# A transformer layer on one core: the second product's weight sums loaded into other buffers, the first pairs' vector work and the last row tiles put in another order

## The chip, the cores and the metric

The kernel runs on one core of a Trainium2 chip. A core has a matrix engine (TensorE, PE in the profile, with its weight loads as PEld), a vector engine (VectorE, DVE), an engine for activations and copies (ScalarE, ACT), a general engine (GpSimd, POOL) and a queue engine (SyncE, SP) that here only issues DMAs. Each engine carries out its own list of instructions strictly in the order in which they were put there; engines wait for each other on semaphores. The metric is the device time of one execution in microseconds.

## The reference

One encoder layer over 512 positions of width 1024, all in float32. A normed input goes through one large projection, a gMLP branch and a dilated attention branch, both merged through gates and an output projection, with a residual. Then comes the feed-forward part, which is where the change lies:

```python
n2 = rms_norm(h, norm_mlp_pre[l])
hid = jnp.square(jax.nn.relu(jnp.einsum('bsd,df->bsf', n2, w_up[l])))
mlp_out = jnp.einsum('bsf,fd->bsd', hid, w_down[l])
h = h + rms_norm(mlp_out, norm_mlp_post[l])
```

`w_up` is 1024 x 4096 and `w_down` is 4096 x 1024. The output is h, 512 x 1024.

## The kernel before, in words

**Float32 by three products.** The matrix engine works on a rounded float32 type. Each operand is split into a high part, a rounded copy made by ScalarE (line 79), and a low part, the difference, made by VectorE (line 80; both in `split_into`). A product of two split operands is three matmuls: high x high, high x low, low x high (`mm3`, `acc3`, and the loop in `product`). So each operand costs one ACT and one DVE pass before PE may use it.

**Seven products in place of eight.** Most of the work is done on 2 x 2 blocks by a seven-product scheme (Winograd's form): sums and differences of blocks are made on VectorE, seven block products run on PE, and results are combined ("joined") on VectorE out of the accumulators. PE saves an eighth of the work, VectorE gets more of it.

**The up projection** (lines 878 to 1006). The normed rows of row tile t are transposed and split by `turn(t)`; its last DVE instruction is returned, and the one of the last call is `turned`. Two pairs of 128-wide feature tiles are computed in the plain way (`up_half`, lines 850 and 922 to 926). The other pairs, i = 2 to 15, use seven products. The four block sums of the moving operand (lines 934 to 937) and their splits `nt[2]`, `nt[1]`, `nt[3]`, `nt[4]` (line 941) are made once; the low part of `nt[4]` is made by GpSimd, the others by VectorE. For each pair, `prep(i)` loads 1 MB of weights into a two-deep ring (`raw_up`, line 911), makes sums in the tile `s` (lines 948, 949, 954; one buffer) and splits `s12`, `ar`, `a12`, `s34`. Then the loop issues the products 6, (the previous pair's 4, in `tail`), 1, 5, 2, 7, 3. Product 7 needs `nt[3]`, product 4 needs `nt[4]`, product 2 needs `a12`, products 1 and 4 need `ar`. Accumulators are copied out or joined at lines 987 to 1005. The last join of the stage is the DVE instruction at line 1002 of the last pair's `tail`.

**The down projection** (from line 1009). The 32 hidden tiles are the contraction. Tiles 0 to 15 are done plainly, two at a time by `plain(f2, order)`: 1 MB of `w_down` into the ring `dnw` of two buffers (tag `raw`, the same ring as the up weights), two splits of it into the ring `hl` of five buffers, 48 matmuls. Tiles 16 to 31 form two chunks c for the seven-product scheme. Order in the code: `plain(0)`, `plain(1)`, `plain(2)`, `first_sums(0)`, `plain(3)`, `first_sums(1)`, `plain(4)`, then the products on chunks, `plain(5)` to `plain(7)`, more products. `first_sums(c)` loads two weight blocks of 1 MB each through the same ring (`block`, line 1052), writes their difference into `tsum[c]` by two DVE instructions (line 1083, in `two`), and makes two sums of hidden blocks (lines 1088 and 1090). `two` serves at lines 1109 and 1171 too, where `tsum[c]` gets further sums.

**The end** (lines 1161 to 1189). The last chunk's products finish row tiles 2 and 3 (accumulators Y) and 0 and 1 (X), 12 matmuls per row tile. For each, `finish` squares with a running sum on ACT (line 1158; the square itself is thrown away into the output tile `o`), multiplies by the gain on DVE (1159), forms the root on GpSimd (96), and writes `o` by two DVE instructions (1153) and two DMAs (1155). The pool of `o` has two buffers, so that the tiles of rows 0 and 1 take over those of rows 2 and 3. The pool `n2pool` has eight buffers of 4 KB per partition: the early moving operands, and behind them `gain`, `s2`, `v`, `t1` and `h2`.

**Who sets the order.** The program is written in one order, and a planner with its own cost estimates picks for each engine, among the instructions that it takes to be ready, the one that stands first in the program. `tc.issue_after(x)` forces instructions of the block that run on x's engine to stand behind x in that engine's list; it adds no wait between engines and does not touch DMAs that another engine issues. Buffers of a pool are handed to a new tile when the planner has seen the old one freed, and the first write then waits for the last reader.

Of the kernel before, what the change touches and what calls it, by code (L numbers as in the profile page):

```python
# [36 lines left out]
def block_kernel(ctx: ExitStack, tc: tile.TileContext, x, norm_mix_pre, w_in, b_gate, ln_v_gain, ln_v_bias,  # L37
# [40 lines left out]
    def split_into(hi, lo, src, sub=nc.vector):  # L78
        nc.scalar.activation(hi, src, AF.Copy)  # L79
        return sub.tensor_tensor(lo, src, hi.bitcast(F32), op=ALU.subtract)  # L80
# [775 lines left out]
    for t in range(4):  # L856
# [18 lines left out]
        r = rstd_of(ss, 1.0 / D)  # L875
        for hs in halves:
            nc.scalar.activation(xn[:, hs], h2[:, hs], AF.Copy, scale=r)
    stds = []
    for w in early:
        stds.append((psB.tile([P, S], F32, name="pu", tag="acc", bufs=4), *w))  # L880
        with tc.issue_after(final.ins):
            final = up_half(*stds[-1], 0)
        with tc.issue_after(final.ins):
            turned = turn(len(stds) + 1)
    wo.close()
    rst.close()
    mst.close()
# [45 lines left out]
    with tc.issue_after(turned.ins):  # L933
        nc.vector.tensor_tensor(fe[:, :, A], fe[:, :, A], fe[:, :, B], op=ALU.subtract)
        nc.vector.tensor_tensor(fe[:, :, B], fo[:, :, B], fe[:, :, B], op=ALU.subtract)
        nc.vector.scalar_tensor_tensor(fo[:, :, B], fe[:, :, A], -1.0, fo[:, :, B], op0=ALU.mult, op1=ALU.subtract)
        nc.vector.scalar_tensor_tensor(fo[:, :, A], fo[:, :, B], -1.0, fo[:, :, A], op0=ALU.mult, op1=ALU.subtract)
        nt = {}
        for nm, src in ((2, fo[:, :, B]), (1, fe[:, :, A]), (3, fe[:, :, B]), (4, fo[:, :, A])):
            nt[nm] = [n2_tile() if nm == 4 else tpool.tile([P, KH, 256], F32R, name="nt", tag="nt") for _ in range(2)]  # L940
            split_into(*nt[nm], src, nc.gpsimd if nm == 4 else nc.vector)
    hst.close()
    hidb = pool(back, "hidb", side="right")

    def prep(i):
        raw = raw_up(i).rearrange("p (j h) (r c) -> p j (h r) c", h=2, r=2)
        s = upool.tile([P, KH, 4, P], F32, name="s", bufs=1)
        nc.vector.tensor_tensor(s[:, :, 0:4:2], raw[:, :, 1:3], raw[:, :, 0:1].to_broadcast([P, KH, 2, P]), op=ALU.add)
        nc.vector.tensor_tensor(s[:, :, 3], s[:, :, 2], raw[:, :, 1], op=ALU.add)  # L949
        s12 = split_back(s[:, :, 2:4], [KH, 2, P])  # L950
        ar = split_back(raw[:, :, 1:3], [KH, 2, P])
        a12 = [upool.tile([P, KH, P], F32R, name="a12" + z) for z in "hl"]
        split_into(*a12, raw[:, :, 3])
        nc.vector.tensor_tensor(s[:, :, 1], s[:, :, 3], raw[:, :, 3], op=ALU.add)
        s34 = split_back(s[:, :, 0:2], [KH, 2, P])
        pick = lambda g, m: [z[:, :, m] for z in g]
        return {1: pick(ar, 0), 2: a12, 3: pick(s34, 1), 4: pick(ar, 1), 5: pick(s12, 0), 6: pick(s12, 1), 7: pick(s34, 0)}
# [16 lines left out]
    for i in range(NSTD, KF // 2):  # L974
# [1 line left out]
        if f % 8 == 0:  # L976
            hid.append((hida if f < 24 else hidb).tile([P, 8, S], F32, name="hid"))
        c2, c1 = hid_of(f), hid_of(f + 1)
        with nullcontext() if i > NSTD else tc.issue_after(turned.ins):
            w = prep(i)  # L980
        Y, Z, X = half_bank("acc"), half_bank("acc"), half_bank("tp")
        product(6, Y, w, True)
        if tail:
# [15 lines left out]

        def tail(w=w, Y=Y, p1=p1, c2=c2, f=f):  # L1000
            product(4, Y, w, False)
            nc.vector.scalar_tensor_tensor(c2[:, :256], Y, -1.0, p1, op0=ALU.mult, op1=ALU.subtract)
            both = hid[f // 8][:, f % 8:f % 8 + 2]
            nc.scalar.activation(both, both, AF.Relu)
            nc.scalar.activation(both, both, AF.Square)
    tail()
    up.close()

    dpool = pool(dn, "dpool", bufs=3)
# [69 lines left out]
    s2 = []  # L1079

    def two(out, x, y, op):
        for i in range(0, 4, 2):
            nc.vector.tensor_tensor(out[:, i:i + 2], x[:, i:i + 2], y[:, i:i + 2], op=op)

    def first_sums(c):
        b22, b12 = block(c, 1, 1), block(c, 0, 1)
        two(tsum[c], b22, b12, ALU.subtract)
        nc.vector.tensor_tensor(a21[c], a11[c], a21[c], op=ALU.subtract)
        s2.append(n2pool.tile([P, 4, 256], F32, name="s2", tag="n2"))
        nc.vector.tensor_tensor(s2[c], a22[c], a21[c], op=ALU.subtract)  # L1090

    first_sums(0)
    plain(3, order)
    first_sums(1)
    plain(4, y_first)
    keep = hida.tile([P, 8, S], F32, name="hid")
    p1, r22, r12, z0 = [keep[:, 2 * i:2 * i + 2] for i in range(4)]
# [71 lines left out]
    for c in range(2):  # L1169
        b21 = block(c, 1, 0)  # L1170
        two(tsum[c], b21, tsum[c], ALU.subtract)
        h4, w4 = h_split(a22[c]), w_split(tsum[c])
        h, w = h_split(a12[c]), w_split(b21)
        if c:
            break
        for i in range(2):
            piece(Y, h4, w4, i)
            piece(X, h, w, i)
    for ps, (hh, hl), ws, ts in ((Y, h4, w4, (2, 3)), (X, h, w, (0, 1))):
        for t in range(2):  # L1180
            for j in range(4):
                wh, wl = ws[j // 2]
                acc3(ps[t], (hh[:, j, tsl[t]], hl[:, j, tsl[t]]), (wh[:, j % 2], wl[:, j % 2]), False, j == 3)
            o = lpool.tile([P, D], F32, name="o")
            if ps is Y:
                nc.vector.tensor_tensor(p1[:, t], Y[t], p1[:, t], op=ALU.add)
                finish(2 + t, [p1[:, t], None], [p1[:, t], r22[:, t]], o, sums[2 + t])
# [45 lines left out]
```

## Time and profile before

| | us |
|---|---|
| three timed runs | 800.35, 801.00, 801.66 (median 801.0) |
| the profiled execution | 800.84 |
| its span, first to last instruction | 799.0 |
| PE busy | 782.7 (98%) |
| DVE busy | 590.9 (74%) |
| ACT busy | 441.9 (55%) |
| POOL busy | 60.4 (8%) |
| granted TensorE clock, mean | 0.995 |

Times in the views are microseconds from the start of the span. A row of the timeline gives start, duration, engine, line, operation, output<-inputs, shapes and how many instructions were merged; what stands in brackets is how long the engine was idle before and what ended that. A row of a DMA-issuing queue (SPq) gives the issue, not the transfer. Matmul rows overlap, since matmuls are pipelined: a 512-column matmul is listed with 0.39 us, and a new one starts every 0.23 us.

### The profile page before, as it was taken

The page shows a single profiled execution, that of the slowest core. Times are in us where ns is not written, and L with a number is a line of the kernel's source. Part 1 is how long each engine was busy: PE and PEld are TensorE (multiplying, and loading weights), DVE is VectorE, ACT ScalarE, POOL GpSimd, SP SyncE. Part 2 cuts the span into 40 slices and gives each one's busy share as a digit, 9 for nine tenths or more (in the row PEclk, how much of TensorE's full clock was granted, in tenths as well). Part 3 has the DMA queues.
Part 4 walks back from the last instruction along what each step waited for, and adds up shares of the span by engine and source line. Part 5 has one row for each costly group of instructions (what it writes and reads, how often), then busy time and mean ns, then how long its engine had stood idle before and what let it go on. Part 6 is the DMA issues. An engine that isn't in the chain of part 4 may idle for free.

```text
span 799.0 us, 12247 instructions
## 1 busy us (share of the span) xinstructions
PE 782.7 (98%) x4869; PEld 710.5 (89%) x4869; DVE 590.9 (74%) x956; ACT 441.9 (55%) x731; POOL 60.4 (8%) x86
## 2 busy tenths in 40 slices
PE   9999999999999999999999999999999999999994
PEld 6899999998988889999988899999999887888883
DVE  6784679978664878788656489988888546896686
ACT  6351467978686554455435457666667424543551
POOL 2300100010104400000001102000000000000001
PEclk9999999999999999999999999999999999999998
DMA  9633733352525433353356222433333354233302
GB/s 324 220 108 107 209 106 106 83 156 75 174 96 137 140 80 107 81 147 89 132 185 202 89 80 82 131 106 106 107 106 129 109 210 159 71 141 131 132 1 105
DMA packets 93706, 101.01 MB, mean 126 GB/s; under 512 B 2721, under 2 KB 74433, under 8 KB 93650
## 3 DMA queue, kind: packets, MB, share of 16 engines
q1 hardware_dynamic: 83312, 79.70, 32.0%
q0 software_dynamic: 10336, 20.54, 8.4%
q8 instruction: 38, 0.62, 0.3%
q14 instruction: 18, 0.15, 0.1%
q10 hardware_dynamic: 2, 0.00, 0.0%
HBM read 90.27 MB, written 9.96 MB: 125 GB/s over the span
## 4 chain that ended last, share of the span: by engine, by line
PE 88%; DVE 5%; DMA 3%; ACT 2%; issue 1%; POOL 0%; DVEq 0%; POOLq 0%; ACTq 0%
PE pacc L965 12%; PE pg L343 9%; PE pgacc L343 6%; PE pd L1032 5%; PE pd L1033 5%; PE pf L84 5%; PE pd L1034 5%; PE pf L85 5%; PE pf L86 5%; PE ptp L965 5%; PE pv L84 4%; PE pv L86 4%; PE pv L85 4%; PE pgS L343 3%; DMA dnw<-in_w_down_dram 2%; PE pd L86 2%
## 5 line engine op out<-in xcount | busy, mean ns | idle before, releaser
L1033 PE MATMUL pd<-hl,hhl 128*128 128x512 f32 x240 | 93.2, 389 | 0.0
L1034 PE MATMUL pd<-hl,hhl 128*128 128x512 f32 x240 | 91.3, 389 | 0.0
L1032 PE MATMUL pd<-hl,hhl 128*128 128x512 f32 x240 | 88.7, 390 | 1.6 <-ACT hl L79 1.6
L965 PE MATMUL pacc<-nt,hl 128*128 128x256 f32 x504 | 66.7, 279 | 1.4 <-DVE nt L80 1.4
L965 PEld LDWEIGHTS pacc<-nt,hl 128*128 128x128 f32 x504 | 62.2, 188 | 1.6 <-DVE nt L80 1.6
L1032 PEld LDWEIGHTS pd<-hl,hhl 128*128 128x128 f32 x240 | 45.0, 188 | 11.2 <-ACT hl L79 2.0
L1034 PEld LDWEIGHTS pd<-hl,hhl 128*128 128x128 f32 x240 | 45.1, 188 | 9.4
L1033 PEld LDWEIGHTS pd<-hl,hhl 128*128 128x128 f32 x240 | 45.1, 188 | 9.2
L79 ACT ACTIVATE hl<-dnw 128x1024 fp32r<-128x1024 f32 x28 | 29.3, 1054 | 41.0 <-PE pd L1034 17.1
L80 DVE TENSOR_TENSOR hl<-dnw,hl 128x1024 fp32r<-128x1024 f32 x28 | 33.9, 1222 | 16.0 <-ACT hl L79 16.0
L74 ACT ACTIVATE hi<-s 128x1024 fp32r<-128x1024 f32 x30 | 31.7, 1059 | 23.8 <-DVE s L330 10.4
L965 PE MATMUL pacc<-n,hl 128*128 128x256 f32 x336 | 44.7, 279 | 0.0
L84 PE MATMUL pf<-nh,hi 128*128 128x512 f32 x112 | 44.5, 397 | 0.0
L85 PE MATMUL pf<-nl,hi 128*128 128x512 f32 x112 | 43.9, 392 | 0.0
L86 PE MATMUL pf<-nh,lo 128*128 128x512 f32 x112 | 43.9, 392 | 0.0
L75 DVE TENSOR_TENSOR lo<-s,hi 128x1024 fp32r<-128x1024 f32 x30 | 36.6, 1223 | 9.7 <-ACT hi L74 9.6
L965 PEld LDWEIGHTS pacc<-n,hl 128*128 128x128 f32 x336 | 41.7, 188 | 0.1
L79 ACT ACTIVATE hl<-s 128x1024 fp32r<-128x1024 f32 x28 | 29.6, 1056 | 21.9 <-DVE s L949 15.6
L80 DVE TENSOR_TENSOR hl<-s,hl 128x1024 fp32r<-128x1024 f32 x28 | 34.2, 1221 | 6.2 <-ACT hl L79 6.2
L85 PE MATMUL pv<-lo,nh 128*128 128x512 f32 x96 | 38.2, 397 | 0.0
L86 PE MATMUL pv<-hi,nl 128*128 128x512 f32 x96 | 37.6, 396 | 0.0
L84 PE MATMUL pv<-hi,nh 128*128 128x512 f32 x96 | 37.4, 397 | 0.0
(387 smaller groups left out, 2221.2 us busy)
## 6 DMA issues: line engine op xcount, KB each, us to landing
dnw<-in_w_down_dram SPq DMA_DIRECT2D x18, 1024.0 KB, 4.8
upw<-in_w_up_dram SPq DMA_DIRECT2D x16, 1024.0 KB, 5.5
qkw<-in_w_in_dram SPq DMA_DIRECT2D x24, 512.0 KB, 5.2
gw<-in_w_in_dram SPq DMA_DIRECT2D x16, 512.0 KB, 5.3
slab<-in_w_in_dram SPq DMA_DIRECT2D x6, 1024.0 KB, 8.8
wow<-in_w_out_dram SPq DMA_DIRECT2D x4, 1024.0 KB, 4.9
w0raw<-in_w_in_dram SPq DMA_DIRECT2D x4, 512.0 KB, 6.4
v0d<-v POOLq DMA_DIRECT2D x4, 512.0 KB, 4.5
```

The costliest lines, as they stand in the source:

```text
L74: nc.scalar.activation(hi, raw, AF.Copy)
L75: (sub or nc.vector).tensor_tensor(lo, raw, hi.bitcast(F32), op=ALU.subtract)
L79: nc.scalar.activation(hi, src, AF.Copy)
L80: return sub.tensor_tensor(lo, src, hi.bitcast(F32), op=ALU.subtract)
L84: nc.tensor.matmul(ps, ah, bh, start=start, stop=False)
L85: nc.tensor.matmul(ps, ah, bl, start=False, stop=False)
L86: return nc.tensor.matmul(ps, al, bh, start=False, stop=stop)
L343: nc.tensor.matmul(ps, a[:, j], b[:, j], start=first and not (j or i), stop=(j == KH - 1 and i == 2), skip_group_check=True)
L965: nc.tensor.matmul(ps, a[:, j], b[:, j], start=first and not (j or m), stop=(j == KH - 1 and m == 2), skip_group_check=True)
L1032: nc.tensor.matmul(ps, ah, bh, start=start, stop=False, skip_group_check=True)
L1033: nc.tensor.matmul(ps, ah, bl, start=False, stop=False, skip_group_check=True)
L1034: return nc.tensor.matmul(ps, al, bh, start=False, stop=stop, skip_group_check=True)
```

## The change

Four edits, in the order of the program.

1. The start of the seven-product up projection. The first sum of the first such pair (line 948, i = 2) may stand on DVE as early as behind the first of the two late `turn` calls; the rest of its `prep` stays behind the second. All DVE work of pair 3's `prep` stands behind the low part of `nt[3]`. For pairs 3 and 4 the split of `ar` is written ahead of that of `s12`. The low part of `nt[4]` is made by VectorE.
2. `first_sums`: one weight block is loaded straight into `tsum[c]`, the other in two halves into two tiles of `n2pool`; neither passes through the `dnw` ring. All its DVE instructions are placed behind the last join of the up projection. The DMAs are issued by SP and are not placed by this.
3. `two` is one DVE instruction over 2048 columns per partition where there were two over 1024.
4. The end: the 12 matmuls of each row tile of the last chunk stand behind those of the row tile before (rows 2, 3, 0, 1), and the output tiles of rows 0 and 1 come from `n2pool`.

```diff
--- before.py
+++ after.py
@@ -875,13 +875,14 @@
         r = rstd_of(ss, 1.0 / D)
         for hs in halves:
             nc.scalar.activation(xn[:, hs], h2[:, hs], AF.Copy, scale=r)
-    stds = []
+    stds, turns = [], []
     for w in early:
         stds.append((psB.tile([P, S], F32, name="pu", tag="acc", bufs=4), *w))
         with tc.issue_after(final.ins):
             final = up_half(*stds[-1], 0)
         with tc.issue_after(final.ins):
-            turned = turn(len(stds) + 1)
+            turns.append(turn(len(stds) + 1))
+    turned = turns[-1]
     wo.close()
     rst.close()
     mst.close()
@@ -938,17 +939,25 @@
         nt = {}
         for nm, src in ((2, fo[:, :, B]), (1, fe[:, :, A]), (3, fe[:, :, B]), (4, fo[:, :, A])):
             nt[nm] = [n2_tile() if nm == 4 else tpool.tile([P, KH, 256], F32R, name="nt", tag="nt") for _ in range(2)]
-            split_into(*nt[nm], src, nc.gpsimd if nm == 4 else nc.vector)
+            low = split_into(*nt[nm], src)
+            if nm == 3:
+                low3 = low
     hst.close()
     hidb = pool(back, "hidb", side="right")
 
     def prep(i):
         raw = raw_up(i).rearrange("p (j h) (r c) -> p j (h r) c", h=2, r=2)
         s = upool.tile([P, KH, 4, P], F32, name="s", bufs=1)
-        nc.vector.tensor_tensor(s[:, :, 0:4:2], raw[:, :, 1:3], raw[:, :, 0:1].to_broadcast([P, KH, 2, P]), op=ALU.add)
+        with tc.issue_after((turns[0] if i == NSTD else low3).ins) if i < NSTD + 2 else nullcontext():
+            nc.vector.tensor_tensor(s[:, :, 0:4:2], raw[:, :, 1:3], raw[:, :, 0:1].to_broadcast([P, KH, 2, P]), op=ALU.add)
+        with tc.issue_after((turned if i == NSTD else low3).ins) if i < NSTD + 2 else nullcontext():
+            return prep_rest(raw, s, NSTD < i < NSTD + 3)
+
+    def prep_rest(raw, s, ar_first):
+        ar = split_back(raw[:, :, 1:3], [KH, 2, P]) if ar_first else None
         nc.vector.tensor_tensor(s[:, :, 3], s[:, :, 2], raw[:, :, 1], op=ALU.add)
         s12 = split_back(s[:, :, 2:4], [KH, 2, P])
-        ar = split_back(raw[:, :, 1:3], [KH, 2, P])
+        ar = ar or split_back(raw[:, :, 1:3], [KH, 2, P])
         a12 = [upool.tile([P, KH, P], F32R, name="a12" + z) for z in "hl"]
         split_into(*a12, raw[:, :, 3])
         nc.vector.tensor_tensor(s[:, :, 1], s[:, :, 3], raw[:, :, 3], op=ALU.add)
@@ -976,8 +985,7 @@
         if f % 8 == 0:
             hid.append((hida if f < 24 else hidb).tile([P, 8, S], F32, name="hid"))
         c2, c1 = hid_of(f), hid_of(f + 1)
-        with nullcontext() if i > NSTD else tc.issue_after(turned.ins):
-            w = prep(i)
+        w = prep(i)
         Y, Z, X = half_bank("acc"), half_bank("acc"), half_bank("tp")
         product(6, Y, w, True)
         if tail:
@@ -999,11 +1007,12 @@
 
         def tail(w=w, Y=Y, p1=p1, c2=c2, f=f):
             product(4, Y, w, False)
-            nc.vector.scalar_tensor_tensor(c2[:, :256], Y, -1.0, p1, op0=ALU.mult, op1=ALU.subtract)
+            joined = nc.vector.scalar_tensor_tensor(c2[:, :256], Y, -1.0, p1, op0=ALU.mult, op1=ALU.subtract)
             both = hid[f // 8][:, f % 8:f % 8 + 2]
             nc.scalar.activation(both, both, AF.Relu)
             nc.scalar.activation(both, both, AF.Square)
-    tail()
+            return joined
+    joined = tail()
     up.close()
 
     dpool = pool(dn, "dpool", bufs=3)
@@ -1079,19 +1088,23 @@
     s2 = []
 
     def two(out, x, y, op):
+        nc.vector.tensor_tensor(out, x, y, op=op)
+
+    def first_sums(c):
+        nc.sync.dma_start(tsum[c], w7[c, 0, :, :, halves[1]])
         for i in range(0, 4, 2):
-            nc.vector.tensor_tensor(out[:, i:i + 2], x[:, i:i + 2], y[:, i:i + 2], op=op)
-
-    def first_sums(c):
-        b22, b12 = block(c, 1, 1), block(c, 0, 1)
-        two(tsum[c], b22, b12, ALU.subtract)
+            b22 = n2pool.tile([P, 2, 512], F32, name="b22", tag="n2")
+            nc.sync.dma_start(b22, w7[c, 1, :, i:i + 2, halves[1]])
+            nc.vector.tensor_tensor(tsum[c][:, i:i + 2], b22, tsum[c][:, i:i + 2], op=ALU.subtract)
         nc.vector.tensor_tensor(a21[c], a11[c], a21[c], op=ALU.subtract)
         s2.append(n2pool.tile([P, 4, 256], F32, name="s2", tag="n2"))
         nc.vector.tensor_tensor(s2[c], a22[c], a21[c], op=ALU.subtract)
 
-    first_sums(0)
+    with tc.issue_after(joined.ins):
+        first_sums(0)
     plain(3, order)
-    first_sums(1)
+    with tc.issue_after(joined.ins):
+        first_sums(1)
     plain(4, y_first)
     keep = hida.tile([P, 8, S], F32, name="hid")
     p1, r22, r12, z0 = [keep[:, 2 * i:2 * i + 2] for i in range(4)]
@@ -1176,12 +1189,14 @@
         for i in range(2):
             piece(Y, h4, w4, i)
             piece(X, h, w, i)
+    final = None
     for ps, (hh, hl), ws, ts in ((Y, h4, w4, (2, 3)), (X, h, w, (0, 1))):
         for t in range(2):
-            for j in range(4):
-                wh, wl = ws[j // 2]
-                acc3(ps[t], (hh[:, j, tsl[t]], hl[:, j, tsl[t]]), (wh[:, j % 2], wl[:, j % 2]), False, j == 3)
-            o = lpool.tile([P, D], F32, name="o")
+            with tc.issue_after(final.ins) if final else nullcontext():
+                for j in range(4):
+                    wh, wl = ws[j // 2]
+                    final = acc3(ps[t], (hh[:, j, tsl[t]], hl[:, j, tsl[t]]), (wh[:, j % 2], wl[:, j % 2]), False, j == 3)
+            o = lpool.tile([P, D], F32, name="o") if ps is Y else n2pool.tile([P, D], F32, name="o2", tag="n2")
             if ps is Y:
                 nc.vector.tensor_tensor(p1[:, t], Y[t], p1[:, t], op=ALU.add)
                 finish(2 + t, [p1[:, t], None], [p1[:, t], r22[:, t]], o, sums[2 + t])
```

## The prediction

> **What bounds the kernel now.** I read first the page, then the list of what the matrix engine waited for, then the timeline around the few places that this list names. Page and list:
>
> ```profile
> span 799.0 us, 12247 instructions
> PE 782.7 (98%) x4869; PEld 710.5 (89%) x4869; DVE 590.9 (74%) x956; ACT 441.9 (55%) x731; POOL 60.4 (8%) x86
> ...
> PE pd L1032 <- ACT hl L79: 1.6, 1, 1.6
> PE pacc L965 <- DVE nt L80: 1.4, 1, 1.4
> ```
>
> The reader is to see that PE sets the time: it is busy for 782.7 of 799.0 us, and only two waits of over a microsecond are listed after the kernel's first microseconds. A change that makes no matmul go away can win only at these two places and where PE isn't running at all, at the end. VectorE, at 74% on average, matters where it is late for PE. I take the three places in turn. All positions are those of the execution before.
>
> **The end.** Timeline of the last microseconds:
>
> ```profile
> 779.05 2.36 DVE L80 TENSOR_TENSOR hl<-dnw,hl 128x1024 fp32r<-128x1024 f32 x2
> 782.94 0.39 PE L1034 MATMUL pd<-hl,hhl 128*128 128x512 f32 x1
> 783.37 0.69 DVE L1186 TENSOR_TENSOR hid<-pd,hid 128x512 f32<-128x512 f32 x1 [0.44 <-PE pd L1034]
> ...
> 787.70 0.39 PE L1033 MATMUL pd<-hl,hhl 128*128 128x512 f32 x1
> 787.93 0.39 PE L1034 MATMUL pd<-hl,hhl 128*128 128x512 f32 x1
> 789.62 0.60 ACT L1158 ACTIVATE o<-pd 128x512 f32<-128x512 f32 x1 [4.80 <-DMA out_dram<-o]
> 790.34 0.69 DVE L1159 TENSOR_TENSOR y<-pd,gain 128x512 f32<-128x512 f32 x1 [1.60 <-ACT o L1158]
> 790.98 0.60 ACT L1158 ACTIVATE o<-pd 128x512 f32<-128x512 f32 x1 [0.67 <-DMA out_dram<-o]
> 792.49 0.74 DVE L1153 SCALAR_TENSOR_TENSOR o<-hid,rs_out,h 128x512 f32<-128x512 f32 x1
> 793.16 0.68 DVE L1159 TENSOR_TENSOR y<-pd,gain 128x512 f32<-128x512 f32 x1
> 795.30 0.75 DVE L1153 SCALAR_TENSOR_TENSOR o<-hid,rs_out,h 128x512 f32<-128x512 f32 x1
> ```
>
> The last matmul ends at 787.93 + 0.39 = 788.32. Two things then lie on the path. The square of row tile 0 begins only at 789.62, because its output buffer `o` is still being sent out (the bracket names the DMA). And the tail of a row tile is gone through twice: the first from 789.62 to 792.49 + 0.74 = 793.23, which is 3.61 us, and the second, whose multiply starts at 793.16, up to 795.30 + 0.75 = 796.05.
>
> The change removes both. With `o` from another pool there is no DMA to wait for: a reader of an accumulator starts about 0.04 us after the matmul that ends at 782.94 + 0.39 (row of 783.37), so the square of the last tile starts at 788.36. With row tiles one by one, a tile takes 12 matmuls at 0.23 us (787.70 to 787.93), 2.7 us, so tile 0 is complete at 785.6, and its tail of 3.61 us ends at 789.25 under and just behind the last matmuls. Tile 1's tail then ends at 788.36 + 3.61 = 791.97, plus 0.1 because its multiply, due at 789.08 (0.72 after the square, as in 790.34 - 789.62), finds VectorE with the end of tile 0's tail. 796.05 - 792.07 = 3.98. What follows the last DVE instruction (796.05 to 799.0: the DMA and the close) stays as it is.
>
> Costs here: PE must now do the row tiles in a fixed order, so an operand that comes late can't be stepped around. Rows 0 and 1 begin 24 matmuls before the end, at 788.16 - 24 x 0.226 = 782.7; their last split ends at 779.05 + 2.36 = 781.41. The spare 1.3 us takes one instruction of 0.69 us (the joins of rows 2 and 3 move ahead) without harm and two of them almost. Bounds 0 and 0.7; I take 0.03, near nothing, by that row. The two tiles more in `n2pool` find buffers that `t1` and `s2` have left; their last readers are 20 us and more ahead. **3.95 us.**
>
> **The stall before `plain(4)`.** Timeline and one window:
>
> ```profile
> 630.48 0.42 DVE L1002 SCALAR_TENSOR_TENSOR hid<-pacc,p 128x256 f32<-128x256 f32 x1 [1.83 <-PE pacc L965]
> 631.57 1.23 DVE L80 TENSOR_TENSOR hl<-dnw,hl 128x1024 fp32r<-128x1024 f32 x1 [0.67 <-ACT hl L79]
> ...
> 636.88 1.22 DVE L1088 TENSOR_TENSOR hid<-hid 128x1024 f32<-128x1024 f32 x1
> 638.01 1.22 DVE L80 TENSOR_TENSOR hl<-dnw,hl 128x1024 fp32r<-128x1024 f32 x1
> ...
> 644.40 2.36 DVE L1083 TENSOR_TENSOR tsum<-dnw 128x1024 f32<-128x1024 f32 x2 [4.03 <-DMA dnw<-in_w_down_dram]
> 660.04 2.36 DVE L1083 TENSOR_TENSOR tsum<-dnw 128x1024 f32<-128x1024 f32 x2 [1.83 <-DMA dnw<-in_w_down_dram]
> 662.43 0.37 SPq L1039 DMA_DIRECT2D dnw<-in_w_down_dram  x1
> 666.34 0.39 PE L1034 MATMUL pd<-hl,hhl 128*128 128x512 f32 x1
> 667.19 2.00 ACT L79 ACTIVATE hl<-dnw 128x1024 fp32r<-128x1024 f32 x2 [10.24 <-DMA dnw<-in_w_down_dram]
> 668.30 2.14 PE L1032 MATMUL pd<-hl,hhl 128*128 128x512 f32 x8 [1.57 <-ACT hl L79]
> ...
> 640.00:668.30 28.30, 26.73 (x118) 21.79 (x118) 9.84 (x10) 5.24 (x6) 0.00 (x0) 1.00 0.57 210
> ```
>
> The matmul of 666.34 should have been followed at 666.57; the next came at 668.30, so 1.73 us are lost. Followed back: the split waits for a load, the load was issued at 662.43, right when the sums of 660.04 (+ 2.36) gave their ring buffer back, and those had waited for their own load. Two buffers carry the plain weights and the blocks of both sums in turn, each load behind a DVE step. The window's columns are PE, PEld, DVE, ACT, POOL: VectorE is busy for 9.84 of 28.3 us, so work isn't what is short there.
>
> With the blocks out of the ring, four loads of it fall away ahead of `plain(4)`. Its load is issued as soon as the second split of `plain(2)`, 638.01 + 1.22, has freed a buffer: 639.3 instead of 662.4, 23 us earlier against a delay of 1.73. The loads that are moved (one whole and two halves per chunk, the same bytes) stand in SP's list ahead of `plain(3)` and `plain(4)`. The four half tiles take buffers that the first, second and third products of the last pair leave, and the join of 630.48 stands behind the last of all products, so SP is held at most until then; `plain(3)` and `plain(4)` then still land well before 655 and 666.
>
> Cost: both hidden sums of chunk 0 (line 1088 and 1090) and two weight sums per chunk now stand behind 630.9, in a stretch where splits for `plain(1)` and `plain(2)` follow each other closely. A sum put into the 0.67 us gap ahead of 631.57 delays that split by 1.22 - 0.67 = 0.55; line 1088's 1.14 already stands ahead of the split of 638.01, so a sum in its place adds nothing, two would add 1.14. Bounds: 0 and 1.7 (both). I take 0.08, near nothing: the planner places a split ahead of a sum whenever it holds the split for ready. **1.65 us.**
>
> **The start of the seven-product pairs.** Timeline, and the group of GpSimd's other low parts:
>
> ```profile
> 469.49 0.69 DVE L843 TENSOR_TENSOR n2f<-pt,cols 128x512 f32<-128x512 f32 x1 [1.35 <-PE pt L842]
> 475.27 1.29 DVE L80 TENSOR_TENSOR a12l<-upw,a12h 128x512 fp32r<-128x512 f32 x2
> 485.17 1.56 PE L965 MATMUL pacc<-nt,hl 128*128 128x256 f32 x12
> 486.13 4.12 POOL L80 TENSOR_TENSOR n<-n2f,n 128x1024 fp32r<-128x1024 f32 x1 [21.34 <-ACT n L79]
> 486.68 1.07 ACT L79 ACTIVATE nt<-n2f 128x1024 fp32r<-128x1024 f32 x1
> 486.85 0.50 PE L965 MATMUL ptp<-n,a12h 128*128 128x256 f32 x2
> 488.24 3.09 DVE L80 TENSOR_TENSOR nt<-n2f,nt 128x1024 fp32r<-128x1024 f32 x1
> 488.37 1.57 PE L965 MATMUL pacc<-nt,hl 128*128 128x256 f32 x12
> 491.38 1.55 PE L965 MATMUL pacc<-nt,hl 128*128 128x256 f32 x11 [1.44 <-DVE nt L80]
> 492.77 1.56 PE L965 MATMUL pacc<-n,hl 128*128 128x256 f32 x12
> 494.17 0.63 PE L965 MATMUL pacc<-nt,hl 128*128 128x256 f32 x4
> ...
> L75 POOL TENSOR_TENSOR lo<-uw,hi 128x1024 fp32r<-128x1024 f32 x4 | 9.6, 2389 | 25.9 <-ACT hi L74 25.8
> ```
>
> Twelve matmuls take 494.17 - 492.77 = 1.40. The twelve from 488.37 were done at 489.77, the next came at 491.38: 1.61 lost, waiting for the low part of `nt[3]`. The twelve from 485.17 were done at 486.57, the next came at 486.85: 0.28 lost. Together 1.89. The low part of `nt[3]` took 3.09 instead of 1.22 us, and it ended (491.33) 1.08 after GpSimd's low part of `nt[4]` did (490.25); GpSimd's took 4.12 where the same shape takes 2.39 elsewhere. The two held each other up.
>
> The change takes from VectorE ahead of `nt[3]`: pair 2's first sum, 1.14 (such an instruction holds VectorE for 1.13 to 1.14, as from 636.88 to 638.01), which fits the 1.35 us gap ahead of 469.49; pair 3's half of the 1.29 us row, 0.6; pair 3's first sum, another 1.14; and 3.09 - 1.22 = 1.87 of mutual hold-up: 4.75 in all. ACT's high part ends at 486.68 + 1.07 = 487.75 even if nothing ahead of it moves, so the low part is there by 489.0 at the latest, and PE asks for it at 489.77. The 1.61 go.
>
> What is late next is pair 3. Its first sum (1.14), second sum (0.6), ACT's high part of `s12` (1.06) and the low part (1.22) now follow 489.0: 493.0, with the low part of `nt[4]` (1.14, moved from GpSimd) under ACT's step. PE reaches pair 3 at 494.17 - 1.61 = 492.56. It can take product 4 of pair 2 first; if not, it waits 0.4, and 1.6 if `ar` comes in between with another 1.14. Should everything have moved up with VectorE, nothing is lost. Bounds 0 and 1.6; I take 0.29, by the first of these. **1.6 us.**
>
> **One sum where there were two.** A sum over 2048 columns takes as long as its two halves, but its first half is ready 1.14 later.
>
> ```profile
> 678.50 2.36 DVE L1083 TENSOR_TENSOR tsum<-tsum,dnw 128x1024 f32<-128x1024 f32 x2
> 685.96 1.04 ACT L79 ACTIVATE hl<-tsum 128x1024 fp32r<-128x1024 f32 x1
> ```
>
> The split that reads chunk 0's sum starts at 685.96, 5 us after even chunk 1's sum has ended (680.86). I take 0; the bound is 4 x 1.14 = 4.6, if that distance were gone for both chunks at both lines. The Trainium skill (Perfetto Trace Analysis, Optimizing Scalar/DVE Operations) speaks against this edit: where Vector isn't saturated but makes other engines idle, breaking instructions up may let work complete sooner. By it the time would be 798.4, by the row 793.8.
>
> **The sum.** 3.95 + 1.65 + 1.6 = 7.2 us, so the profiled execution of 800.84 becomes 793.6. The median of the three runs is 0.16 above it: 801.0 - 7.2 = 793.8.
>
> **The rivals.**
> 1. Pair 3 takes over the stall of pair 2. VectorE keeps all its work and gets 1.14 more; the 1.6 are spent again. 801.0 - 7.2 + 1.6 = 795.4. For it: VectorE had no gap from 473 on; against it: 4.75 us taken away ahead of `nt[3]`.
> 2. The ring's stall returns as a stall of PE on a split behind the new sums at 631 to 640 (cost 1.7), or the planner leaves the load late: 795.4. For it: the gaps there are 0.67 us; against it: only one place has two sums in a row to offer.
> 3. Half of the end is lost: VectorE still has tile 0's tail, or late joins of rows 2 and 3, in hand when tile 1 is done. 795.8. For it: in the row of 793.16 a multiply stood behind another tile's whole tail. Against it: there both tiles were ready together.
> 4. The doubled sums come late, 798.4, as worked out above. This is the skill's rule as a mechanism; the 5 us of distance speak against it.
> 5. Slower: a weight sum stands at the head of VectorE's list while its load hasn't landed, in the place of 636.88, and the split of 638.01 queues behind it. PE asks for that split at about 639.4; a landing at T costs T + 1.2 - 639.4 or so. The 7.2 are used up, and 0.2% (about what a measurement of this kernel can tell from no change, 1.6 us) more, from T = 647. At T = 650 it is 12 us: 805.8. For it: before, the sums waited 4.03 and 1.83 us for loads that landed at 644.4 and 660.0. Against it: these loads had a ring buffer to wait for, the new ones have not.
> 6. It doesn't do what it says: the planner keeps its old order at the ends, 801.
>
> **How the numbers follow.** Forecast 0.60; rivals 1 to 6: 0.12, 0.09, 0.08, 0.03, 0.05, 0.03. The range: below, the costs I took (0.4) come to nothing, and the runs shown lie within 0.65 of their median, so 792.5, and 792.2 with the refilling of PE after the two stalls; above, rivals 1 to 3 and two of them at once (795.4 + 1.65 = 797.05, 795.8 + 1.65 = 797.45), so 797.6. Left out are rivals 4 to 6 and what lies at the edges. Faster: 0.60 + 0.12 + 0.09 + 0.08 + 0.03 = 0.92; the same 0.03; slower 0.05.
>
> **What would show it.** Right: no wait of PE over 0.5 us in its list behind the first microseconds; `nt` low parts of 1.2 us each and none on POOL; the load of `plain(4)` some 20 us before PE needs it; an `o2` square within 0.1 us of the last matmul, and 10.7 us from the last matmul's end to the span's end (799.0 - 788.32) turned into 6.7. Wrong step by step: a PE wait on `hl` or `n` at pair 3; a PE wait at 631 to 640, or DVE idle for a DMA there; DVE busy with rows 2, 3 or 0 when the last square ends. A single PE wait over 8 us would make the whole forecast wrong.

## The result and the profile after

| | before | after |
|---|---|---|
| timed, median | 801.6 us (6 runs, 800.35 to 801.91) | 796.2 us (6 runs, 795.37 to 797.5) |
| the profiled execution | 800.84 | 795.91 |
| its span | 799.0 | 794.1 |

The ratio is 0.9938, with a 95% interval from 0.9925 to 0.9951: 4 to 6 us faster. The forecast was 793.8, so the direction and the range hold, and by the profiled executions a third of the gain is missing (4.9 us for 7.2). Three places were to give it. One view for each, and first the page and the list of PE's waits of after:

```profile
span 794.1 us, 12232 instructions
PE 782.3 (99%) x4869; PEld 710.5 (89%) x4869; DVE 590.1 (74%) x953; ACT 443.3 (56%) x731; POOL 56.8 (7%) x85
...
PE pacc L974 <- DVE u L996: 0.6, 1, 0.6
...
PE ptp L974 <- ACT p L995: 0.3, 1, 0.3
```

The two waits of over a microsecond are gone, and two smaller ones that were not there before stand in the seven-product pairs. Timeline of PE around the place of the old stall, and its last matmul:

```profile
665.95 0.39 PE L1043 MATMUL pd<-hl,hhl 128*128 128x512 f32 x1
666.17 0.39 PE L1041 MATMUL pd<-hl,hhl 128*128 128x512 f32 x1
...
785.63 0.39 PE L1043 MATMUL pd<-hl,hhl 128*128 128x512 f32 x1
```

These are the same matmuls as those of 666.34, 668.30 and 787.93 before (counted along PE's list). They divide the 4.9 us of the span: what is gained up to the first (the start), from the first to the last (the stall), and behind it (the end).

| | forecast | after | how |
|---|---|---|---|
| start of the pairs | 1.6 | 0.39 | 666.34 - 665.95 |
| stall ahead of `plain(4)` | 1.65 | 1.91 | (787.93 - 666.34) - (785.63 - 665.95) |
| end | 3.95 | 2.60 | 10.68 - (794.1 - 786.02) |

The stall went whole: 1.73, and 0.18 in which PE takes up its pace again, which the forecast's sum had left out. VectorE's sums stand in the stretch that the prediction named, and no matmul waits for them. Timeline of DVE, with the issue of `plain(4)`'s load from SP's:

```profile
629.63 0.42 DVE L1010 SCALAR_TENSOR_TENSOR hid<-pacc,p 128x256 f32<-128x256 f32 x1 [1.82 <-PE pacc L974]
629.97 2.35 DVE L1098 TENSOR_TENSOR tsum<-b,tsum 128x1024 f32<-128x1024 f32 x2
632.24 1.22 DVE L1099 TENSOR_TENSOR hid<-hid 128x1024 f32<-128x1024 f32 x1
...
642.56 0.37 SPq L1048 DMA_DIRECT2D dnw<-in_w_down_dram  x1
```

The end, timeline of DVE, ACT and POOL:

```profile
781.22 0.68 DVE L1172 TENSOR_TENSOR hid<-hid,gain 128x512 f32<-128x512 f32 x1
783.25 2.74 DVE L1166 SCALAR_TENSOR_TENSOR o<-hid,rs_out,h 128x512 f32<-128x512 f32 x4 [0.39 <-POOL rs_out L96]
785.90 0.68 DVE L1172 TENSOR_TENSOR y<-pd,gain 128x512 f32<-128x512 f32 x1
786.77 0.69 DVE L1172 TENSOR_TENSOR y<-pd,gain 128x512 f32<-128x512 f32 x1
789.43 0.74 DVE L1166 SCALAR_TENSOR_TENSOR o<-hid,rs_out,h 128x512 f32<-128x512 f32 x1
...
783.33 0.60 ACT L1171 ACTIVATE o<-pd 128x512 f32<-128x512 f32 x1 [1.27 <-PE pd L1043]
786.05 0.60 ACT L1171 ACTIVATE o<-pd 128x512 f32<-128x512 f32 x1 [2.03 <-PE pd L1043]
...
739.75 0.53 POOL L1158 DMA_DIRECT2D h<-h2d  x1 [1.41 <-DVE hl L80]
783.70 0.57 POOL L1158 DMA_DIRECT2D h<-h2d  x1
```

and from the DMA view of the end (name, count, size of one, median us from issue to landing):

```profile
out_dram<-o SPq DMA_DIRECT2D x8, 256.0 KB, 4.1
```

The last square starts 0.03 us after the last matmul's end (786.02), as forecast. But the multiply of row tile 0, whose square is done at 783.9, comes only at 785.90: VectorE has the four output instructions of rows 2 and 3 in hand, in one go. From the last square to the end of the last output instruction (790.17) it takes 4.12 us, where 3.71 were forecast. Then come 3.93 us to the end of the span, where before there were 2.95. The DMA view says where to look: output transfers land a median 4.1 us after their issue, before 2.1. And one of the four residual loads, 512 KB, is issued at 783.70 among them; before, all four were issued by 747.5. The median hides two groups: in the trace the first four outputs, with that load among them, land after 4.1 to 4.3 us, the last four after 2.6 to 2.7, and before, all eight took 2.0 to 2.2.

The start, timeline of ACT, DVE and PE:

```profile
507.37 0.63 ACT L79 ACTIVATE a12h<-upw 128x512 fp32r<-128x512 f32 x1 [1.93 <-DMA upw<-in_w_up_dram]
508.03 0.69 DVE L80 TENSOR_TENSOR a12l<-upw,a12h 128x512 fp32r<-128x512 f32 x1 [0.55 <-ACT a12h L79]
509.24 0.42 DVE L996 TENSOR_TENSOR u<-pacc,p 128x256 f32<-128x256 f32 x1
509.81 1.66 PE L974 MATMUL pacc<-nt,hl 128*128 128x256 f32 x12 [0.59 <-DVE u L996]
```

and two links of the chain of waits (start, duration, what):

```profile
493.63 5.49 DMA upw<-in_w_up_dram
501.89 5.45 DMA upw<-in_w_up_dram
```

Product 7 adds to the accumulator that `u` (the code's `u2`) must have read first. VectorE is free at 507.5 (the join of 507.06 takes 0.42), but the low part of `a12` of the pair **after the next** (this `u` is pair 4's, the low part pair 6's, counted along VectorE's list) stands ahead of `u` in that list, that one waits for ACT's high part, and ACT for a load of weights issued at 501.89. A load that nobody needs yet thus holds PE up by 0.75 us. The chain of waits names this load. Before the change, the same two instructions stood the other way round:

```profile
508.56 0.42 DVE L988 TENSOR_TENSOR u<-pacc,p 128x256 f32<-128x256 f32 x1 [0.35 <-ACT p L987]
...
513.86 0.68 DVE L80 TENSOR_TENSOR a12l<-upw,a12h 128x512 fp32r<-128x512 f32 x1
```

A second loss, 0.47 us at 518.84, follows in the next pair (PE for `p`).

### The profile page after: what moved, and what is told of

The parts are those of the page before. It is cut to its first block, busy times and chain, and to the rows that moved or that the text cites. A ratio compares the mean times of both kernels' runs of the same rounds, so it can differ in the third digit from the quotient of the medians.

```text
span 794.1 us, 12232 instructions
## 1 busy us (share of the span) xinstructions
PE 782.3 (99%) x4869; PEld 710.5 (89%) x4869; DVE 590.1 (74%) x953; ACT 443.3 (56%) x731; POOL 56.8 (7%) x85
## 4 chain that ended last, share of the span: by engine, by line
PE 94%; ACT 2%; DMA 1%; DVE 1%; issue 0%; DVEq 0%; ACTq 0%
PE pacc L974 10%; PE pg L343 9%; PE pd L1041 7%; PE pd L1042 7%; PE pd L1043 7%; PE pgacc L343 6%; PE pf L84 5%; PE pf L85 5%; PE pf L86 5%; PE ptp L974 4%; PE pv L84 4%; PE pv L86 4%; PE pv L85 4%; PE pgS L343 3%; PE pd L85 2%; PE pd L84 2%
## 5 line engine op out<-in xcount | busy, mean ns | idle before, releaser
L1042 PE MATMUL pd<-hl,hhl 128*128 128x512 f32 x240 | 93.2, 389 | 0.0
L1041 PE MATMUL pd<-hl,hhl 128*128 128x512 f32 x240 | 92.3, 389 | 0.0
L1043 PE MATMUL pd<-hl,hhl 128*128 128x512 f32 x240 | 91.1, 389 | 0.0
```

The source lines that it names most:

```text
L1041: nc.tensor.matmul(ps, ah, bh, start=start, stop=False, skip_group_check=True)
L1042: nc.tensor.matmul(ps, ah, bl, start=False, stop=False, skip_group_check=True)
L1043: return nc.tensor.matmul(ps, al, bh, start=False, stop=stop, skip_group_check=True)
```

## The experiments

Each is the changed kernel, or the one before, with one thing different (the fifth and the last combine two); the times of before are those measured beside it.

| kernel | median | before | ratio (95%) |
|---|---|---|---|
| first edit alone | 800.1 | 800.8 | 0.9989 (0.998 to 0.9998) |
| second and third alone | 798.4 | 800.8 | 0.997 (0.9961 to 0.998) |
| fourth alone | 797.5 | 800.8 | 0.9961 (0.9946 to 0.9976) |
| residual loads early | 796.1 | 800.8 | 0.9934 (0.9914 to 0.9955) |
| and row 3 behind row 2 | 795.8 | 801.5 | 0.9928 (0.9914 to 0.9943) |
| `a12` behind `u2` | 794.7 | 801.5 | 0.9912 (0.9898 to 0.9927) |
| no spare output buffers | 799.1 | 801.5 | 0.9969 (0.9956 to 0.9981) |
| spare buffers, no row order | 798.1 | 801.5 | 0.9953 (0.9938 to 0.9968) |
| `ar` as before | 796.0 | 802.6 | 0.9919 (0.9899 to 0.9938) |
| `nt[4]` on GpSimd | 797.5 | 802.6 | 0.9937 (0.9918 to 0.9956) |
| `two` in halves | 797.9 | 802.6 | 0.994 (0.992 to 0.9959) |
| `a12` and residual loads | 793.7 | 802.6 | 0.9892 (0.9875 to 0.9909) |

Two executions of the same work can differ by about 1.2 us in the up projection alone. One window, in which PE is never idle, of before and of the fourth edit alone, whose work there is the same; PE's column is its busy time and its matmuls, the last but two is the granted clock:

```profile
520.00:580.00 60.00, 60.00 (x517) 60.00 (x516) 51.20 (x73) 39.09 (x57) 0.00 (x0) 1.00 0.34 106
```

```profile
520.00:580.00 60.00, 60.00 (x512) 60.00 (x511) 50.88 (x73) 38.52 (x56) 0.00 (x0) 1.00 0.34 106
```

PE starts 1% fewer matmuls at the same listed clock of 1.00. So gains under 1 us are read from the places, not from the times.

**The three edits one by one.**

> The kernel before with the first edit alone (order of the first pairs' sums and low parts). Theory from the profile after: the two stalls of before (0.28 and 1.61 us) go, but about 0.2 + 0.75 + 0.47 us come back as waits of the first seven-product pairs, so the gain is 0.5 us, within 0.2 to 0.8. Rival (the prediction's term): 1.6 us. A second rival: the edit is worth its 1.6 us by itself and the waits of 509 and 518 us come from another edit; then this run shows no wait there.

Measured: the matmul of 666.34 comes at 666.00, so the start alone gains 0.34, and the waits of 509.8 and 518.8 are there (0.70 and 0.54 lost). They belong to the first edit. What no theory had: the stall ahead of `plain(4)` shrinks to 0.71 as well. Timeline rows of this kernel:

```profile
629.23 0.42 DVE L1010 SCALAR_TENSOR_TENSOR hid<-pacc,p 128x256 f32<-128x256 f32 x1 [4.09 <-PE pacc L974]
...
660.92 0.37 SPq L1047 DMA_DIRECT2D dnw<-in_w_down_dram  x1
...
666.00 0.39 PE L1042 MATMUL pd<-hl,hhl 128*128 128x512 f32 x1
666.94 2.11 PE L1040 MATMUL pd<-hl,hhl 128*128 128x512 f32 x8 [0.55 <-ACT hl L79]
```

The last join of the stage comes 1.25 us sooner (630.48 before), the chain of sums and loads behind it moves with it, and the load is issued at 660.92 instead of 662.43. Of the 1.25, only 0.34 are the start; in PE's list, four plain matmuls fewer (28 for 32, 0.23 us each) stand ahead of the last pair's final product, so most of this gain comes from the planner's order.

> The kernel before with the second and third edit alone (weight sums from spare buffers, one sum where there were two). Theory from the profile after: the stall ahead of the fifth plain step goes wholly, gain 1.8 us, no new wait of PE. Rival (the prediction's fourth): the doubled sums come late and give back up to 4.6 us. The prediction's term is 1.65.

Measured: no wait at the place of the stall (667.08, then 667.31), 119.45 us from there to the last matmul as in the changed kernel: 1.9 us. The first edit's microsecond there and this one are the same, which is the larger part of why the three edits' medians alone add up to 6.5 us, while the whole change brings 5.4 by the medians and 4.9 by the spans.

> The kernel before with the fourth edit alone (row tiles one by one, spare buffers for the last two output tiles). Theory: the stretch from the last matmul's end to the span's end goes from 10.7 to about 8.1 us, as in the changed kernel, gain 2.6. Prediction's term: 6.7 us, gain 3.95. If this run shows less than 7.2, then the second edit, by its hold of the spare buffers, is what delays row 1's residual load and bunches the output DMAs; if it shows about 8, the fourth edit itself is.

Measured: the last matmul starts at 788.89, so the end is 797.0 - 789.28 = 7.7 us. The residual load of row 1 is late here too (786.95), so the fourth edit delays it, not the second; 7.7 is nearer to the 8 of that reading. The 0.4 us between this kernel's 7.7 and the changed kernel's 8.08 belong to the second edit, as is worked out below.

**The end.** The residual loads first:

```diff
+    h2s = {}
+    for t in (2, 3, 0, 1):
+        h2s[t] = n2pool.tile([P, D], F32, name="h2", tag="n2")
+        nc.gpsimd.dma_start(h2s[t], h2d[tsl[t]])
...
-        h2 = n2pool.tile([P, D], F32, name="h2", tag="n2")
-        nc.gpsimd.dma_start(h2, h2d[tsl[t]])
+        h2 = h2s[t]
```

> The changed kernel with the four residual loads (h2, 512 KB each) allocated and issued ahead of the last chunk's products, where row 1's was issued at 783.7 us amid the output DMAs. Theory (the late load slows the output DMAs): the outputs land nearer to 2.1 us after issue than to 4.1, the last one 0.5 us or more sooner, time 0.5 to 1.0 us below the changed kernel's (795.2 to 795.7 in its terms). Rival (the eight output DMAs slow each other, since rows come 2.7 us apart): landing times stay at 4 us, time the same within 0.3.

Measured, DMA view of the end:

```profile
out_dram<-o SPq DMA_DIRECT2D x8, 256.0 KB, 2.1
```

The outputs are back at 2.1 us and the end takes 794.6 - 787.03 = 7.57: half a microsecond gained where it was expected. The median (796.1, the changed kernel's 796.2) doesn't show it. The profiled execution, the longest of this kernel's four, is one of those with 512 matmuls in the window above; how the other three ran there is not on record.

> The changed kernel with the residual loads ahead of the last chunk (as in x4_h2_early) and with row tile 3's join placed on DVE behind the start of row tile 2's root. Theory (the tails of rows 2 and 3 come bunched on VectorE and delay row 0's): row 2's output comes before row 3's multiply, row 0's multiply starts at most 1.4 us after its square where it was 2.57 (785.90 - 783.33), the last DVE instruction starts about 0.4 us sooner after the last square (2.9 to 3.0 us instead of 3.38), and the stretch from the last matmul's end to the span's end comes to 7.2, from 7.57. Rival (row 1's own tail of 3.6 us is what ends last, whatever rows 2 and 3 do): the distance stays 3.38 and the end 7.57. By time alone the 0.4 us can't be told; the profile decides.

```diff
-                nc.vector.tensor_tensor(p1[:, t], Y[t], p1[:, t], op=ALU.add)
+                with tc.issue_after(rooted[-1].ins) if t else nullcontext():
+                    nc.vector.tensor_tensor(p1[:, t], Y[t], p1[:, t], op=ALU.add)
```

(`rooted` holds the `rs_in` instructions of line 93.) Measured, DVE:

```profile
785.01 0.69 DVE L1178 TENSOR_TENSOR y<-pd,gain 128x512 f32<-128x512 f32 x1
785.78 1.42 DVE L1172 SCALAR_TENSOR_TENSOR o<-hid,rs_out,h 128x512 f32<-128x512 f32 x2
787.11 0.75 DVE L1172 SCALAR_TENSOR_TENSOR o<-y,rs_out,h 128x512 f32<-128x512 f32 x1
787.77 0.75 DVE L1172 SCALAR_TENSOR_TENSOR o<-hid,rs_out,h 128x512 f32<-128x512 f32 x1
788.44 0.69 DVE L1178 TENSOR_TENSOR y<-pd,gain 128x512 f32<-128x512 f32 x1
```

Row 0's multiply did come 0.72 us after its square (784.29). But row 1's now stands behind row 0's outputs, 1.43 us after its square, and VectorE waits 0.73 us for its root: 3.58 us from the last square to the start of the last output instruction (the theory's rival said 3.38), 7.73 in all. The theory fell as far as the gain goes: VectorE has no gap from 784.3 to 789.2 here, and what one row gains in that list another loses.

> The changed kernel with the output tiles of rows 0 and 1 from the two-buffer pool again: the order of row tiles without the spare buffers. Theory (the spare buffers carry nearly all of the fourth edit): row 0's square waits for row 2's output DMA, which lands about 787 in the changed kernel's times, so the last two tails start 3.5 us later and the end is 10.2 to 11.5 us after the last matmul where it is 8.08: 2.1 to 3.4 us slower than the changed kernel. Rival (the order carries half): under 1.6 us slower.

Measured: the last matmul ends at 785.85, the span at 796.5: 10.65 us, as before the change. The first square waits for an output DMA, and all four residual loads are early again:

```profile
786.71 0.60 ACT L1171 ACTIVATE o<-pd 128x512 f32<-128x512 f32 x1 [4.82 <-DMA out_dram<-o]
...
744.98 0.53 POOL L1158 DMA_DIRECT2D h<-h2d  x1 [4.86 <-DVE hhl L80]
```

So the order of rows without the buffers is worth nothing, and the output tiles taken from `n2pool` are what makes row 1's load late.

> The changed kernel without the order of the row tiles, with the spare output buffers. Theory: both last tiles are complete within half a microsecond, their squares, multiplies and four output instructions come one behind the other on VectorE, last DVE instruction about 5.3 us after the last square begins where it is 4.12 with the order, end 8.2 to 9.2: the order is worth 0.2 to 1.1 us. The prediction counted the last tile's own tail alone (3.61), so by it the order is worth a whole second tail of 2.8 us and more.

Measured: 796.3 - 787.41 = 8.89 us. With the buffers, the order is worth another 0.8 us, within the 0.2 to 1.1 of the theory and far from a whole tail.

**The start.** VectorE's low part of `a12` behind `u2` of the pair before, for the first four such pairs:

```diff
-        split_into(*a12, raw[:, :, 3])
+        with tc.issue_after(u2s[-1].ins) if 0 < len(u2s) <= 4 else nullcontext():
+            split_into(*a12, raw[:, :, 3])
...
-        nc.vector.tensor_tensor(u2, Y, p1, op=ALU.add)
+        u2s.append(nc.vector.tensor_tensor(u2, Y, p1, op=ALU.add))
```

> The changed kernel, with VectorE's low part of a12 of a pair placed behind u2 (line 996) of the pair before, for the first four such pairs. Theory (the first edit's gain is eaten by an in-order wait: u2 stands behind a low part whose load lands late): the wait of PE for u (0.75 us lost at 509.8) goes, the one for p (0.47 at 518.8) stays or moves, PE reaches 547 about 0.7 us sooner than in the changed kernel. Rival (VectorE simply has too much work there, 25.3 us busy of the 28 from 490 on): the loss comes back within 10 us at another product.

Measured, ACT and DVE:

```profile
506.58 0.42 DVE L999 TENSOR_TENSOR u<-pacc,p 128x256 f32<-128x256 f32 x1
506.92 0.68 DVE L80 TENSOR_TENSOR a12l<-upw,a12h 128x512 fp32r<-128x512 f32 x1
507.22 0.64 ACT L79 ACTIVATE a12h<-upw 128x512 fp32r<-128x512 f32 x1 [1.91 <-DMA upw<-in_w_up_dram]
```

ACT waits for the load as long as before; `u` doesn't any more, and its row stands 2.7 us sooner. PE's list has neither the wait for `u` nor that for `p`. The matmul of 666.34 comes at 664.52 and the median is 794.7. So VectorE, busy nearly all of that time, was not short. The second wait went with the first; whether as its result, or because the edit also orders the pairs behind, this run can't tell.

How much the load decides is seen in the kernel with `two` in halves, whose start is that of the changed kernel. Chain of waits:

```profile
501.96 6.50 DMA upw<-in_w_up_dram
```

and timeline of ACT, DVE and PE:

```profile
508.49 0.63 ACT L79 ACTIVATE a12h<-upw 128x512 fp32r<-128x512 f32 x1 [3.18 <-DMA upw<-in_w_up_dram]
...
509.15 0.69 DVE L80 TENSOR_TENSOR a12l<-upw,a12h 128x512 fp32r<-128x512 f32 x1 [1.59 <-ACT a12h L79]
...
510.93 1.29 PE L974 MATMUL pacc<-nt,hl 128*128 128x256 f32 x9 [1.84 <-DVE u L996]
```

The same 1 MB took 6.50 us in place of 5.45 in this execution, and PE's wait grew from 0.59 to 1.84, by a little more than the load did.

> The changed kernel with the split of ar behind that of s12 for all pairs, as before the change. Theory (what costs the later pairs 0.75 and 0.47 us is a12's low part ahead of u2 in VectorE's list, and the early ar only shifts the planner's order): with another order the waits of 509.8 and 518.8 go and the first pairs gain 0.5 to 1.2 us. Rival (the early ar is what lets product 4 of pair 3 run in time): PE waits up to 1.1 us for hl in pair 3 or 4 and nothing is gained.

```diff
-            return prep_rest(raw, s, NSTD < i < NSTD + 3)
+            return prep_rest(raw, s, False)
```

Measured: the wait of 509.8 is gone; instead PE loses 0.2 at 492.7, 0.2 at 517.7 and 0.4 at 518.6, where 1.2 were lost in all in the changed kernel. No product of pairs 3 and 4 waited for `ar`. In VectorE's list the low part of pair 6 stands behind `u` of pair 4 again (513.94 and 508.40), as before the change. So it was the early split of `ar` that led the planner to put it ahead. The gain, about 0.5 us by these places, lies at the lower end of what the theory said, and not all waits went.

> The changed kernel with the low part of nt[4] on GpSimd again, as before. Theory (GpSimd and VectorE hold each other up: 4.12 us against 2.39, and 3.09 against 1.22, before): the low part that runs beside it on VectorE takes 2 to 3 us again. If it is the low part of nt[3], PE waits for it up to 1.6 us again and this move carries the first edit's gain; if it is pair 3's work, the wait moves there. Rival (the reordering alone clears the place): both durations as before the change but no wait of PE, and VectorE's 1.14 us less work takes some of the 0.75 away: same time or up to 0.5 better.

```diff
-            low = split_into(*nt[nm], src)
+            low = split_into(*nt[nm], src, nc.gpsimd if nm == 4 else nc.vector)
```

Measured, POOL, DVE and PE:

```profile
485.62 2.41 POOL L80 TENSOR_TENSOR n<-n2f,n 128x1024 fp32r<-128x1024 f32 x1 [21.14 <-ACT n L79]
...
486.52 2.59 DVE L80 TENSOR_TENSOR nt<-n2f,nt 128x1024 fp32r<-128x1024 f32 x1 [1.15 <-ACT nt L79]
...
491.44 1.44 PE L974 MATMUL ptp<-n,hl 128*128 128x256 f32 x10 [0.48 <-DVE hl L80]
```

The low part of `nt[3]` takes 2.59 us where it takes 1.22 in the changed kernel, and PE loses 0.65 us at pair 3's product 1, whose operand is split behind it on VectorE; there it loses nothing. So the move away from GpSimd carries 0.65 us of what this place gained, the new order the rest. The Trainium skill (SBUF — State Buffer, Who interferes with whom) says that a VectorE instruction with two SBUF inputs contends with a GpSimd instruction that reads SBUF, and that the port pair they share is an exclusive lock. The trace agrees: GpSimd, issued 0.9 us sooner, ends at 488.03, and VectorE's ends 1.08 us later, about as if it had begun then.

**One sum in place of two.**

> The changed kernel with the sums in `two` in halves again. Prediction's term: 0, no PE wait in either. Rival (the Trainium skill's rule, broken-up instructions let work complete sooner; the prediction's fourth rival): up to 4.6 us faster in halves. A third way: halves let the planner put other work between them, and VectorE's order changes without a wait of PE: the same time within 0.3 us.

```diff
-        nc.vector.tensor_tensor(out, x, y, op=op)
+        for i in range(0, 4, 2):
+            nc.vector.tensor_tensor(out[:, i:i + 2], x[:, i:i + 2], y[:, i:i + 2], op=op)
```

Measured: from the matmul at 668.71 (that of 666.17 after) to the last one at 788.17 there are 119.46 us, as in the changed kernel. The doubled sum costs and brings nothing; the higher median can't be laid on it as far as the trace goes: the profiled execution loses its time at the start, as shown above. The rule of the Trainium skill (Perfetto Trace Analysis, Optimizing Scalar/DVE Operations) is for instructions that leave other engines idle, and none waited for these sums: the trace gives it no case here.

**Both mends together.**

> The changed kernel with both mends: the low parts of a12 behind u2 of the pair before (as in x7_a12) and the residual loads ahead of the last chunk (as in x4_h2_early). Theory (start and end are separate places): no PE wait in the first pairs, output DMAs of 2.1 us, end 7.6 us after the last matmul; 0.4 to 0.5 us below x7_a12, some 794.2 us. Rival (x7_a12's gain and x4's are the same microseconds, or the earlier loads disturb other transfers): the time of x7_a12, 794.7, or above.

Measured, PE:

```profile
664.75 0.39 PE L1046 MATMUL pd<-hl,hhl 128*128 128x512 f32 x1
664.98 0.39 PE L1044 MATMUL pd<-hl,hhl 128*128 128x512 f32 x1
...
784.43 0.39 PE L1046 MATMUL pd<-hl,hhl 128*128 128x512 f32 x1
```

No listed wait of PE in the pairs, output transfers of 2.1 us, the matmul of 666.34 at 664.75, the last one at 784.43, the span 792.4. That is 1.59, 1.91 and 3.10 us for start, stall and end, 6.6 together: the best of all kernels here. Its fastest run is 793.64, that of before beside it 800.46; the ratio in the table is larger because runs of before went up to 804.4 there.

## Why the prediction was right or wrong

The direction was right and the time lies in the range, but 796.2 is nearer to the times of rivals 1 (795.4) and 3 (795.8) than to the forecast of 793.8: the stall came out as said, the start and the end each fell short by over 1 us, and the range took that in. One sum of the range is off: 793.8 less 0.4 and 0.65 is 792.75, not 792.5; nothing here hangs on it.

**The stall ahead of `plain(4)`: right.** The ring was the cause, and with the blocks out of it the load came 20 us sooner (642.56 for 662.43; the forecast 639.3 was early, as it left out the sums that VectorE then does ahead of the split). The cost of 0.08 for crowded sums did not arise. Rivals 2 and 5 are out: no sum waited for its load.

**One sum for two: right,** at 0. Rival 4 is out.

**The start: the stall went, but the term was mis-sized, 0.39 for 1.6.** The step that failed is "what is late next is pair 3". Pair 3 never waited. The step looked one pair ahead, for work that VectorE must do, and rival 1 gave it 1.6 for the same reason. What took the time back was a low part for a pair two further on, put ahead of `u2` in VectorE's list and tied by it to a load of 5.45 us. The order did it: the load itself was issued 2.2 us sooner than before (501.89 for 504.10). The early split of `ar`, meant to help pairs 3 and 4, brought that order, as the kernel with `ar` as before shows; the loss is of rival 1's size, but not its mechanism. A smaller miss in the same step: pair 2's first sum did not go into the gap ahead of 469.49. It stood behind the last transposes, and PE lost 0.2 there:

```profile
469.48 0.69 DVE L843 TENSOR_TENSOR n2f<-pt,cols 128x512 f32<-128x512 f32 x1 [1.34 <-PE pt L842]
...
471.00 1.22 DVE L952 TENSOR_TENSOR s<-upw 128x1024 f32<-128x1024 f32 x1
```

With the mend the start is worth 1.59, so the term was right as what could be had, though partly by luck: the 0.29 set aside for pair 3 were not needed, and the 0.2 just shown were not in the sum.

**The end: right in its mechanism, 2.60 for 3.95.** Two steps failed. The first is "What follows the last DVE instruction (...) stays as it is": it went from 2.95 to 3.93. 0.6 of that are the last output's transfer, 2.64 us from issue to landing where it took 2.04 before: the two tiles taken from `n2pool`, which "find buffers that `t1` and `s2` have left" at no cost, pushed row 1's residual load into the output transfers. With the load moved, it took 2.08 again. The other 0.4 come with the second edit. From the last landing to the end of the span it is 0.9 us in the kernels without that edit (before, first alone, fourth alone) and 1.3 in every kernel with it, also where the outputs are spaced as before (second and third alone, no spare output buffers). The traces show SP closing the program with nine waits in a fixed order. Without the second edit, the last output's wait is the last of the nine; with it, it is the third, and the six behind it take some 0.06 us each. With that edit the kernel issues two DMAs more (171 for 169); that these move the place is likely, but no run shows it by itself.

The second step is the last tail's 3.71, which counted tile 0's work beside it but not that of rows 2 and 3: it took 4.12. That is rival 3, named and then left at 0.08. Why the planner gave row 1's load its late place is not settled.

## What to carry to other kernels

When an edit moves work to take a stall away, follow the in-order lists several steps on, and look above all for an instruction that waits for a later step's data ahead of one that is needed now. A buffer that is free is not free of cost: ask which load would have got it. Even the waits that close the program have an order that an edit elsewhere can change. And edits that are timed alone may each be paid for the same microsecond, so they don't add up.

## What the runs showed of the hardware

- A transfer of 256 KB to memory lands 2.0 to 2.2 us after its issue, also where four are issued within 2 us (residual loads early). With a load of 512 KB issued among them, the first four took 4.1 to 4.3 us and the last four 2.6 to 2.7 in the changed kernel.
- The stretch from the last landing to the end of the span was 0.9 us where the last output's wait stood last in SP's closing list, and 1.3 where six more waits stood behind it.
- The same 1 MB load, at the same place of the program, took 5.45 us in one execution and 6.50 in another, with 6.1 in a third (spare buffers, no row order).
- PE's pace differs by 1% between executions (517 or 512 matmuls of 256 columns in 60 us) at a listed clock of 1.00, for some 125 us (492 to 620); of the 14 traces, seven have the one pace and seven the other. Behind it, with 512 columns, the stretch to the last matmul is 119.45 us in every kernel without the stall. What sets the pace was not found.
